# Two matmuls per weight tile, of 512 and 256 columns, in SwiGLU, output projection and gate of a hybrid trunk on one Trainium2 core

## The chip, the cores and the metric

The program runs on one NeuronCore of a Trainium2 chip. A core has five engines with queues of their own: TensorE (PE) multiplies matrices from SBUF into PSUM, VectorE (DVE) and ScalarE (ACT) read both memories, GpSimd (POOL) is used here on SBUF alone, and SyncE (SP) issues the DMAs. The metric is the device time of one execution in microseconds; lower is better.

## The reference

Two layers of a trunk over 256 tokens and 1024 features, all in float32. Each layer is

```
x += 1/2 SwiGLU_a(RMSNorm(x))              # 1024 -> 2 x 2816 -> 1024
u  = RMSNorm(x) @ W_in                     # 1024 -> 3072, the mixer: 8 heads of attention, Hyena convolution
x += W_out [RMSNorm(y_A) ; RMSNorm(y_B)] * g_out
x += 1/2 SwiGLU_b(RMSNorm(x))
x += sigmoid(RMSNorm(x) @ W_g) * (p[i] @ W_p)
```

and a last RMSNorm follows. `swiglu(h) = (silu(h @ w_gate) * (h @ w_up)) @ w_down`. Weights are read once: 192 MB in all.

## The kernel before

Activations lie transposed: features on the 128 partitions, the 256 tokens (T) in the free dimension, so x is eight tiles x[0..7] of 128x256. A weight matrix comes in tiles of 128x128, sixteen to a DMA of 1 MB (`raw`), in the order in which they are used.

float32 products are made from two rounded parts. Each operand is split into a high part and what remains, the low part: w = wh + wl, x = xh + xl. ACT casts eight weight tiles at a time to wh (L250), DVE subtracts to get wl (L253; in the mixer every third half goes to POOL), and six such halves of 8 tiles are in flight (`WBUFS`). The parts of an activation lie side by side in one tile of 128x512: `hl[:, :T]` high and `hl[:, T:]` low. `mm3` (L164) then issues three matmuls of 256 columns per weight tile, wh·xh, wh·xl and wl·xh (L165, L166, L167), which add up in 256 columns of a PSUM bank. Each matmul loads its weights anew.

PSUM is a pool `ps` of eight banks of 128x512. In SwiGLU a bank holds 256 columns of the gate and 256 of the up product of one block of 128 hidden features; the first two blocks (`heads`) are computed together, column by column of x, in four half-filled banks. 1/rms of the norm is known later than the products: it is spread over all partitions into `rb` and multiplied in on the way out of PSUM (L439 in DVE). Then follow silu on ACT (L442), gate times up on DVE (L445), the high part on ACT (L447) and the low part on DVE (L449). The down projection sums 22 tiles into one bank per column and DVE adds half of it to x (L480). The output projection is done in two parts of four tiles per column, for the attention and the Hyena half; each waits for its own 1/rms (`rna`, `rhy`), is multiplied by it (L886) and added to x (L887, on POOL for the first part, on DVE for the second). `prep` makes the parts xg of the next norm's input (ACT L329, DVE L331) and sums squares (ACT L314, POOL L317).

The order is set in the program: the products go to PE one weight tile after the other, and after every three weight tiles (`TICK`) each live `Fiber` is advanced by one step, so that the rest is recorded in small steps between the products. That order is kept as written on PE and ACT (`ORDERED`); DVE and POOL are ordered by the framework's scheduler. All engines run their queues in order.

Of the kernel before, what the change touches and what calls it, by code (L numbers as in the profile page):

```python
# [11 lines left out]
F32 = mybir.dt.float32  # L12
# [3 lines left out]
ALU = mybir.AluOpType  # L16
AX = mybir.AxisListType

P = 128
# [40 lines left out]
# columns of the packed per-partition parameters of one layer  # L60
# [15 lines left out]
def hybrid_trunk(ctx: ExitStack, tc: tile.TileContext, w, xT, pT, rpb, small, wf, zT, dft, idft, decay, out):  # L76
# [11 lines left out]
    psp = ctx.enter_context(tc.tile_pool(name="ps", bufs=8, space=bass.MemoryType.PSUM))  # L88
# [8 lines left out]

    def bank():
        return psp.tile([P, 512], F32, tag="ps", name=nm("ps"))
# [19 lines left out]
    class Fiber:  # L119
        """Work of several engines, emitted step by step between the products."""  # L120
# [43 lines left out]
    def mm3(o, lh, ll, rh, rl, start, stop):  # L164
        PE.matmul(o, lh, rh, start=start, stop=False)  # L165
        PE.matmul(o, lh, rl, start=False, stop=False)  # L166
        PE.matmul(o, ll, rh, start=False, stop=stop)  # L167
        if not Pace.inside:
            Pace.total += 1
            Pace.count += o.free_size() // T if hasattr(o, "free_size") else o.shape[-1] // T  # L170
            while Pace.count >= TICK:
                Pace.count -= TICK
                tick()

# [21 lines left out]
    # even times, odd times, and the latter's negative; real and imaginary parts  # L196
# [37 lines left out]
    def part(steps=1):  # L234
        """The next 8 weight tiles in their two 12-bit parts."""
        n = Stream.parted
        Stream.parted += 1
        while Stream.loaded < min(n // 2 + 2, DEPTH * PIECES):
            load()
        raw = Stream.raws[n // 2]  # L240
        h = whp.tile([P, HALF, P], F32R, tag="wh", name=nm("wh"))
        l = wlp.tile([P, HALF, P], F32R, tag="wl", name=nm("wl"))
        fb = Fiber(None)
        Stream.ready[n] = (h, l, fb)

        def go():
            k = HALF // steps
            for a in range(0, HALF, k):
                src = raw[:, n % 2 * HALF + a : n % 2 * HALF + a + k]
                S.copy(h[:, a : a + k], src)  # L250
                yield
                e = G if Stream.on_pool and n % Stream.on_pool == 0 else V
                e.tensor_sub(l[:, a : a + k], src, f(h[:, a : a + k]))  # L253
# [39 lines left out]
    class Inputs:  # L293
        """The two parts of g * x of the norm at hand."""
# [5 lines left out]
        def __getitem__(self, c):  # L300
            hl, fb = self.xs[c]
            fb.finish()
            return hl[:, :T], hl[:, T:]

    class Squares:
        """Sum of the squares of `n` blocks, in whatever order they come."""
# [27 lines left out]
    def onward(i, cg, c, before):  # L334
        """After `before`, which brings x[c] up to date, the next norm's input."""
        hl = t2(F32R, "xg")

        def go():
            yield from before
            yield  # L340
            yield from prep(i, cg, c, hl)

        scaled.append((hl, spawn(go())))

    def rsqrt(v):
        """v ** -0.5 of two columns by Newton's steps from the exponent's halving."""
# [18 lines left out]
    class Rstd:  # L365
        """1/rms of each token: `r`, tokens on partitions, and `dst`, on all partitions."""
# [58 lines left out]
    def ffn(i, cg_next, i_next):  # L425
# [5 lines left out]
        def gated(pg, pu, joint, hl):  # L431
            yield from rest(EV)
            yield from rs.wait()
            gu = t2(s="gu")
            if joint is None:
                V.tensor_mul(gu[:, :T], pg, rb)
                V.tensor_mul(gu[:, T:], pu, rb)
            else:
                V.tensor_tensor(v2(gu), v2(joint), rb2(), op=ALU.mult)  # L439
# [5 lines left out]
            V.tensor_mul(a, s, gu[:, T:])  # L445
            yield
            S.copy(hl[:, :T], a)  # L447
            yield
            V.tensor_sub(hl[:, T:], a, f(hl[:, :T]))  # L449
# [5 lines left out]
        heads = [bank()[:, :T] for _ in range(4)]  # L455
        for c in range(KD):
            xh, xl = xs[c]
            for o in heads:
                wh, wl = ws.next()
                mm3(o, wh, wl, xh, xl, c == 0, c == KD - 1)  # L460
        for j in (0, 2):
            start(heads[j], heads[j + 1], None)
        for ff in range(2, NF):
            b = bank()
            for o in (b[:, :T], b[:, T:]):
                product(o, ws, xs)
            start(None, None, b)
        ws = Tiles()
        new_norm()
        for c in range(KD):  # L470
            ps = bank()[:, :T]
            for k in range(NF):
                wh, wl = ws.next()
                hl, fb = act[k]
                fb.finish()
                mm3(ps, wh, wl, hl[:, :T], hl[:, T:], k == 0, k == NF - 1)
# [14 lines left out]
    def filter_steps(i):  # L491
# [96 lines left out]
        # sums and differences of the even and the odd times' spectra  # L588
# [22 lines left out]
    def mixer(i):  # L611
# [3 lines left out]
        def columns(between=None):  # L615
            """Two blocks of 128 columns of u from the next 16 weight tiles."""
# [7 lines left out]
        # values, tokens on partitions  # L624
# [36 lines left out]
        class QK:  # L661
            """Queries and keys of a pair of heads, the queries with zeros for the other head."""
# [25 lines left out]
        class Head:  # L688
            """One head's probabilities: the scores' softmax, then turned over."""
# [56 lines left out]
        def head_norm(src, sq, ch, hl):  # L746
            """The two parts of g * y, and its squares added up."""
# [21 lines left out]
        def conv(b, chans, res):  # L769
            """Short convolution of the two blocks of channels in a bank."""  # L770
# [66 lines left out]
        def spectral(a, ps):  # L837
            """The gated input's spectrum, frequencies on partitions, times the filter's."""
# [34 lines left out]
        def project(wo, c, parts):  # L873
            ps = bank()[:, :T]
            for k in range(4):
# [3 lines left out]
                mm3(ps, wh, wl, hl[:, :T], hl[:, T:], k == 0, k == 3)  # L879
            return ps  # L880

        def add(c, ps, st, e):
            yield from rest(EV)
            yield from st.wait()
            t = t1()
            V.tensor_mul(t, ps, st.dst)  # L886
# [71 lines left out]
    def ple(i, last, given):  # L958
# [22 lines left out]
        def update(c, ps):  # L981
            yield from rest(PLE_EV)
            yield from rs.wait()
            g = t1()
            V.tensor_mul(g, ps, rb)
# [27 lines left out]
        for c in range(KD):  # L1013
            ps = bank()[:, :T]
            product(ps, ws, xs)
# [80 lines left out]
def _rpb_index():  # L1096
    """Where the bias of (token of the query, token of the key) lies; the last place outside the window."""
# [7 lines left out]
def _tiles(wm):  # L1105
    """[K, M] -> [M tiles, K tiles, 128, 128]."""
# [97 lines left out]
```

## Time and profile before

| | us |
|---|---|
| runs | 1114.56, 1114.68, 1115.82 |
| median | 1114.68 |
| span of the profiled execution, first to last instruction | 1112.9 |
| PE busy | 1087.2 |
| DVE busy | 840.5 |
| ACT busy | 600.3 |
| POOL busy | 205.1 |
| mean granted TensorE clock | 0.996 of full |

The profile is one execution; its span leaves out what lies before the first and after the last instruction. In it the gate and up products of layer 0 run from 6 to 140 us, its down projection to 207, the mixer to 306, the output projection to 330, SwiGLU b to 525 and the gated input to 531; layer 1 follows with the same stages, and its last gate product ends at 1100.

In the profile's rows `L253 DVE ... wl<-raw,wh 128x1024` reads: line of the kernel, engine, operation, tile written and tiles read, shape. Timeline rows begin with the start and the duration in us; x2 and above are merged instructions. In the views by stretch each engine's busy time stands beside its number of instructions.

### The profile page before, as it was taken

Reading aid. Unit: us, or ns where it says so; the run is one execution under the profiler, and the core shown is the slowest. Engines: PE = TensorE matmul, PEld = TensorE weight load, DVE = VectorE, ACT = ScalarE, POOL = GpSimd, SP = SyncE. Lnnn points to the kernel's source line nnn. Section 1 sums busy time; section 2 is a strip of 40 time slices with the busy share of each in tenths; the row PEclk is TensorE's granted clock in tenths of the full one; section 3 lists DMA queues with packets and bytes.
Section 4 is the critical chain, followed back from the end, with each engine's and each line's share of the span. In section 5 each row is a group of like instructions: output and inputs, shape, how many; then the busy total and the mean of one; then the engine's idle time right before and its main releaser. Section 6 shows DMA issues by size and latency. Waiting matters only on the chain.

```text
span 1112.9 us, 21462 instructions
## 1 busy us (share of the span) xinstructions
PE 1087.2 (98%) x8828; PEld 1074.4 (97%) x8828; DVE 840.5 (76%) x1352; ACT 600.3 (54%) x1006; POOL 205.1 (18%) x182
## 2 busy tenths in 40 slices
PE   7999999999999999999999999999999999999996
PEld 7999999999999999999999999999989999999995
DVE  4988777798999766655878878677899986665554
ACT  6555455376746444444655455544855554444444
POOL 3000111544362000011100002125433700000111
PEclk9999999999999999999999999999999999999998
DMA  8565455454335555455455554454523464555421
GB/s 319 215 236 201 154 191 186 170 173 169 114 117 197 190 189 190 176 175 183 161 195 200 215 188 174 173 185 152 190 77 114 142 217 183 189 189 186 176 95 39
DMA packets 32994, 194.29 MB, mean 175 GB/s; under 512 B 3584, under 2 KB 6528, under 8 KB 10880
## 3 DMA queue, kind: packets, MB, share of 16 engines
q1 hardware_dynamic: 32896, 192.92, 48.4%
q8 instruction: 69, 1.13, 0.4%
q14 instruction: 29, 0.24, 0.1%
HBM read 191.86 MB, written 1.05 MB: 173 GB/s over the span
## 4 chain that ended last, share of the span: by engine, by line
PE 80%; DVE 11%; ACT 4%; issue 3%; DMA 1%; POOL 1%; SPq 0%; ACTq 0%; DVEq 0%; POOLq 0%
PE ps L166 26%; PE ps L167 26%; PE ps L165 26%; DVE wl L253 2%; ACT wh L250 2%; DMA raw<-in_w 1%; DVE rt L360 1%; DVE s L783 1%; DVE s L886 1%; DVE x L887 1%; ACT t L723 1%; DVE xg L331 0%; POOL acc L317 0%; ACT t L716 0%; DVE y L752 0%
## 5 line engine op out<-in xcount | busy, mean ns | idle before, releaser
L253 DVE TENSOR_TENSOR wl<-raw,wh 128x1024 fp32r<-128x1024 f32 (+1 forms) x328 | 410.9, 1257 | 193.7 <-ACT wh L250 191.7
L250 ACT CAST wh<-raw 128x1024 fp32r<-128x1024 f32 (+1 forms) x350 | 362.0, 1040 | 321.6 <-PE ps L166 226.8
L165 PE MATMUL ps<-xg,wh 128*128 128x256 f32 x1856 | 528.2, 285 | 5.9 <-ACT xg L1032 5.9
L166 PE MATMUL ps<-xg,wh 128*128 128x256 f32 x1856 | 527.5, 284 | 5.4 <-DVE xg L331 5.3
L167 PE MATMUL ps<-xg,wl 128*128 128x256 f32 x1856 | 526.9, 284 | 0.0
L166 PEld LDWEIGHTS ps<-xg,wh 128*128 128x128 f32 x1856 | 357.7, 193 | 7.2 <-DVE xg L331 6.3
L165 PEld LDWEIGHTS ps<-xg,wh 128*128 128x128 f32 x1856 | 357.8, 193 | 6.3 <-ACT xg L1032 5.9
L167 PEld LDWEIGHTS ps<-xg,wl 128*128 128x128 f32 x1856 | 357.7, 193 | 0.0
L167 PE MATMUL ps<-act,wl 128*128 128x256 f32 x704 | 199.4, 283 | 0.0
L165 PE MATMUL ps<-act,wh 128*128 128x256 f32 x704 | 199.4, 283 | 0.0
L166 PE MATMUL ps<-act,wh 128*128 128x256 f32 x704 | 199.4, 283 | 0.0
L317 POOL TENSOR_TENSOR acc<-acc,q 128x256 f32<-128x256 f32 x62 | 65.9, 1064 | 541.2 <-ACT q L314 524.8
L165 PEld LDWEIGHTS ps<-act,wh 128*128 128x128 f32 x704 | 135.2, 192 | 0.4
L166 PEld LDWEIGHTS ps<-act,wh 128*128 128x128 f32 x704 | 135.2, 192 | 0.4
L167 PEld LDWEIGHTS ps<-act,wl 128*128 128x128 f32 x704 | 135.2, 192 | 0.0
L439 DVE TENSOR_TENSOR gu<-ps,rb 128x512 f32<-128x512 f32 x80 | 55.0, 689 | 20.6 <-PE ps L167 19.0
L253 POOL TENSOR_TENSOR wl<-raw,wh 128x1024 fp32r<-128x1024 f32 x22 | 55.0, 2499 | 62.7 <-ACT wh L250 49.9
L566 POOL TENSOR_TENSOR t<-t,t 128x512 f32<-128x512 f32 x4 | 5.7, 1414 | 225.7 <-PE ps L167 121.0
L329 ACT ACTIVATE xg<-x,sm 128x256 fp32r<-128x256 f32 x56 | 28.1, 506 | 33.2 <-DVE x L480 14.0
L397 ACT ACTIVATE s<-ident,rl 128x128 fp32r<-128x128 f32 x24 | 8.3, 395 | 65.4 <-DVE rl L392 65.4
L442 ACT ACTIVATE s<-gu 128x256 f32<-128x256 f32 x88 | 35.9, 414 | 12.8 <-DVE gu L439 12.0
L449 DVE TENSOR_TENSOR act<-s,act 128x256 fp32r<-128x256 f32 x88 | 38.3, 444 | 0.0
(193 smaller groups left out, 1222.7 us busy)
## 6 DMA issues: line engine op xcount, KB each, us to landing
raw<-in_w SPq DMA_DIRECT2D x172, 1024.0 KB, 4.8
bias<-in_rpb SPq DMA_DIRECT2D x16, 256.0 KB, 2.8
raw<-in_w SPq DMA_DIRECT2D x4, 256.0 KB, 4.6
x<-in_xT SPq DMA_DIRECT2D x8, 128.0 KB, 4.8
raw<-in_w SPq DMA_DIRECT2D x2, 512.0 KB, 5.7
t<-in_wf SPq DMA_DIRECT2D x4, 256.0 KB, 5.4
dec<-in_decay SPq DMA_DIRECT2D x4, 256.0 KB, 5.4
out<-o SPq DMA_DIRECT2D x4, 256.0 KB, 2.4
```

The costliest lines, as they stand in the source:

```text
L165: PE.matmul(o, lh, rh, start=start, stop=False)
L166: PE.matmul(o, lh, rl, start=False, stop=False)
L167: PE.matmul(o, ll, rh, start=False, stop=stop)
L250: S.copy(h[:, a : a + k], src)
L253: e.tensor_sub(l[:, a : a + k], src, f(h[:, a : a + k]))
L317: G.tensor_add(self.ac, self.ac, q)
L329: S.activation(hl[:, :T], x[c], AF.Copy, scale=g)
L360: V.tensor_scalar(r[:, c], y[:, c], y[:, c], hv[:, c], op0=ALU.mult, op1=ALU.mult)
L439: V.tensor_tensor(v2(gu), v2(joint), rb2(), op=ALU.mult)
L442: S.activation(s, gu[:, :T], AF.Silu)
L449: V.tensor_sub(hl[:, T:], a, f(hl[:, :T]))
L723: S.activation(e[:, cs], e[:, cs], AF.Copy, scale=ri[:, tt : tt + 1])
```

## The change

A weight tile now takes two matmuls. `mm2` issues wh times the whole 128x512 tile [xh, xl], so that columns 0 to 255 of the bank hold wh·xh and columns 256 to 511 wh·xl, and then adds wl·xh, 256 columns wide, onto the second half. The two halves of the bank are summed on the way out. SwiGLU (gate, up, down), the output projection and the gate of the per-layer input use it; the mixer's columns, values, attention, transforms and the per-layer projection keep `mm3`. The low parts count for nothing less than before: the same three partial products are formed.

```diff
-    psp = ctx.enter_context(tc.tile_pool(name="ps", bufs=8, space=bass.MemoryType.PSUM))
+    psp = ctx.enter_context(tc.tile_pool(name="ps", bufs=4, space=bass.MemoryType.PSUM))
...
+    def pair():
+        return psp.tile([P, 2, 512], F32, tag="ps", name=nm("ps"))
     def bank():
-        return psp.tile([P, 512], F32, tag="ps", name=nm("ps"))
+        if not free:
+            b = pair()
+            free.extend((b[:, 1], b[:, 0]))
+        return free.pop()
...
+    def mm2(b, lh, ll, r, start, stop):
+        PE.matmul(b, lh, r, start=start, stop=False)
+        PE.matmul(b[:, T:], ll, r[:, :T], start=False, stop=stop)
+        paced()
+
+    def halves(dst, b):
+        if len(b.shape) == 3:
+            dst = v2(dst)
+        S.copy(dst, b[..., T:])
+        yield
+        V.tensor_add(dst, dst, b[..., :T])
...
-        def gated(pg, pu, joint, hl):
+        def gated(b, hl):
             yield from rest(EV)
+            gu = t2(s="gu")
+            yield from halves(gu, b)
             yield from rs.wait()
-            gu = t2(s="gu")
-            if joint is None:
-                V.tensor_mul(gu[:, :T], pg, rb)
-                V.tensor_mul(gu[:, T:], pu, rb)
-            else:
-                V.tensor_tensor(v2(gu), v2(joint), rb2(), op=ALU.mult)
+            G.tensor_tensor(v2(gu), v2(gu), rb2(), op=ALU.mult)
+            yield
             yield
             s = t1()
             S.activation(s, gu[:, :T], AF.Silu)
...
             def half_step(c=c, ps=ps):
                 yield from rest(EV)
-                V.scalar_tensor_tensor(x[c], ps, 0.5, x[c], op0=ALU.mult, op1=ALU.add)
+                for b in (ps[:, :T], ps[:, T:]):
+                    V.scalar_tensor_tensor(x[c], b, 0.5, x[c], op0=ALU.mult, op1=ALU.add)
...
         def add(c, ps, st, e):
             yield from rest(EV)
+            t = t1()
+            yield from halves(t, ps)
             yield from st.wait()
-            t = t1()
-            V.tensor_mul(t, ps, st.dst)
+            V.tensor_mul(t, t, st.dst)
             e.tensor_add(x[c], x[c], t)
...
         def update(c, ps):
             yield from rest(PLE_EV)
+            g = t1()
+            yield from halves(g, ps)
             yield from rs.wait()
-            g = t1()
-            V.tensor_mul(g, ps, rb)
+            V.tensor_mul(g, g, rb)
```

PSUM is handed out in four pairs of banks: a block of SwiGLU takes a pair (gate in one bank, up in the other), and `bank()` deals out the halves of a pair one after the other, so that a pair comes free when both halves have been read. The copy of the second half and its sum with the first don't wait for 1/rms; the multiplication by it does, and in SwiGLU it is POOL's.

On PE, in SwiGLU b of layer 0, two weight tiles of one block before the change (ps: PSUM, xg: the parts of g·x, wh and wl: the parts of the weights):

```order
L165 MATMUL ps_5053<-xg_4299,wh_4919 128x256
L166 MATMUL ps_5053<-xg_4299,wh_4919 128x256
L167 MATMUL ps_5053<-xg_4299,wl_4920 128x256
L165 MATMUL ps_5053<-xg_4334,wh_4919 128x256
L166 MATMUL ps_5053<-xg_4334,wh_4919 128x256
L167 MATMUL ps_5053<-xg_4334,wl_4920 128x256
```

and three weight tiles now:

```order
L191 MATMUL ps_4078<-xg_3674,wh_3915 128x512
L192 MATMUL ps_4078<-xg_3674,wl_3916 128x256
L191 MATMUL ps_4078<-xg_3689,wh_3915 128x512
L192 MATMUL ps_4078<-xg_3689,wl_3916 128x256
L191 MATMUL ps_4078<-xg_3714,wh_3915 128x512
L192 MATMUL ps_4078<-xg_3714,wl_3916 128x256
```

The 512 columns of xg pass wh in one matmul; 2368 of 8742 rows of PE are gone.

On DVE, at the same place, a block's work before:

```order
L439 TENSOR_TENSOR gu_5005<-ps_4918,rb 128x512
L253 TENSOR_TENSOR wl_4987<-raw_4804,wh_4986 128x1024
L445 TENSOR_TENSOR s_5032<-s_5019,gu_5005 128x256
L253 TENSOR_TENSOR wl_5022<-raw_4869,wh_5021 128x1024
L449 TENSOR_TENSOR act_4984<-s_5032,act_4984 128x256
```

and now, where gu_4214 goes to POOL (L473, times rb) and then to ACT between its first and its fourth row here:

```order
L201 TENSOR_TENSOR gu_4214<-gu_4214,ps_4146 128x512
L484 TENSOR_TENSOR act_4145<-s_4205,act_4145 128x256
L281 TENSOR_TENSOR wl_4232<-raw_4103,wh_4231 128x1024
L480 TENSOR_TENSOR s_4253<-s_4244,gu_4214 128x256
L484 TENSOR_TENSOR act_4199<-s_4253,act_4199 128x256
```

DVE's multiplication by rb has become the sum of the two halves.

On DVE in the output projection of layer 0, the steps from the first column of the Hyena part to the first xg before (s: the scaled column, rhy: its 1/rms):

```order
L886 TENSOR_TENSOR s_4268<-ps_4216,rhy_2757 128x256
L886 TENSOR_TENSOR s_4271<-ps_4199,rhy_2757 128x256
L887 TENSOR_TENSOR x_86<-x_86,s_4268 128x256
L887 TENSOR_TENSOR x_85<-x_85,s_4271 128x256
L886 TENSOR_TENSOR s_4287<-ps_4236,rhy_2757 128x256
L886 TENSOR_TENSOR s_4304<-ps_4258,rhy_2757 128x256
L887 TENSOR_TENSOR x_87<-x_87,s_4287 128x256
L887 TENSOR_TENSOR x_88<-x_88,s_4304 128x256
L331 SCALAR_TENSOR_TENSOR xg_4235<-x_86,sm,xg_4235 128x256
```

and now:

```order
L201 TENSOR_TENSOR s_3706<-s_3706,ps_3675 128x256
L923 TENSOR_TENSOR s_3694<-s_3694,rhy_2265 128x256
L923 TENSOR_TENSOR s_3706<-s_3706,rhy_2265 128x256
L924 TENSOR_TENSOR x_85<-x_85,s_3694 128x256
L924 TENSOR_TENSOR x_86<-x_86,s_3706 128x256
L201 TENSOR_TENSOR s_3736<-s_3736,ps_3675 128x256
L923 TENSOR_TENSOR s_3736<-s_3736,rhy_2265 128x256
L363 SCALAR_TENSOR_TENSOR xg_3689<-x_86,sm,xg_3689 128x256
```

Each column has one more row (L201), and the product with rhy now reads two tiles in SBUF.

More of the change, by code (lines that the diff above doesn't have):

```diff
@@ L96, in nm @@
         return f"{s}{uid[0]}"
+    free = []
+    def pair():
+        return psp.tile([P, 2, 512], F32, tag="ps", name=nm("ps"))
     def bank():
-        return psp.tile([P, 512], F32, tag="ps", name=nm("ps"))
+        if not free:
+            b = pair()
+            free.extend((b[:, 1], b[:, 0]))
+        return free.pop()
     def t2(dt=F32, s="t"):
@@ L167, in mm3, with paced @@
         PE.matmul(o, ll, rh, start=False, stop=stop)
+        paced(o.free_size() // T if hasattr(o, "free_size") else o.shape[-1] // T)
+    def paced(n=1):
         if not Pace.inside:
             Pace.total += 1
-            Pace.count += o.free_size() // T if hasattr(o, "free_size") else o.shape[-1] // T
+            Pace.count += n
             while Pace.count >= TICK:
@@ L300, in __getitem__, with both @@
         def __getitem__(self, c):
+            hl = self.both(c)
+            return hl[:, :T], hl[:, T:]
+        def both(self, c):
             hl, fb = self.xs[c]
             fb.finish()
-            return hl[:, :T], hl[:, T:]
+            return hl
     class Squares:
@@ L422, in product, with product2 @@
             mm3(o, wh, wl, xh, xl, c == 0, c == KD - 1)
+    def product2(b, ws, xs):
+        for c in range(KD):
+            wh, wl = ws.next()
+            mm2(b, wh, wl, xs.both(c), c == 0, c == KD - 1)
     def ffn(i, cg_next, i_next):
@@ L453, in start @@
             act.append((hl, spawn(gated(*a, hl))))
-        heads = [bank()[:, :T] for _ in range(4)]
+        heads = [pair() for _ in range(2)]
         for c in range(KD):
[L457 to L462, printed above, removed]
+            for b in heads:
+                for j in range(2):
+                    wh, wl = ws.next()
+                    mm2(b[:, j], wh, wl, xs.both(c), c == 0, c == KD - 1)
+        for b in heads:
+            start(b)
         for ff in range(2, NF):
[L464 to L467, printed above, removed]
+            b = pair()
+            for j in range(2):
+                product2(b[:, j], ws, xs)
+            start(b)
         ws = Tiles()
@@ L470, in ffn @@
         for c in range(KD):
-            ps = bank()[:, :T]
+            ps = bank()
             for k in range(NF):
@@ L873, in project @@
         def project(wo, c, parts):
-            ps = bank()[:, :T]
+            ps = bank()
             for k in range(4):
@@ L878, in project @@
                 fb.finish()
-                mm3(ps, wh, wl, hl[:, :T], hl[:, T:], k == 0, k == 3)
+                mm2(ps, wh, wl, hl, k == 0, k == 3)
             return ps
@@ L1013, in ple @@
         for c in range(KD):
-            ps = bank()[:, :T]
-            product(ps, ws, xs)
+            ps = bank()
+            product2(ps, ws, xs)
             if last:
```

2 lines of the change are left out of this document (1 added, 1 removed).

## The prediction

> **What bounds the kernel now.** I read the page first: busy time by engine and the slices, then the chain that ended last.
>
> ```profile
> PE 1087.2 (98%) x8828; PEld 1074.4 (97%) x8828; DVE 840.5 (76%) x1352; ACT 600.3 (54%) x1006; POOL 205.1 (18%) x182
> DVE  4988777798999766655878878677899986665554
> PEclk9999999999999999999999999999999999999998
> PE 80%; DVE 11%; ACT 4%; issue 3%; DMA 1%; POOL 1%; SPq 0%; ACTq 0%; DVEq 0%; POOLq 0%
> ```
>
> TensorE is busy in 98% of the span at nine tenths or more of its clock in every slice but the last; the chain is PE's for 80% and VectorE's for 11%. Busy time of pipelined matmuls says little about what one costs, so next comes the distance from start to start in the timeline of PE: first 256 columns (36 rows, first and last), then 512 columns (32 rows), then two 512s among 256s.
>
> ```profile
> 199.77 0.28 PE L166 MATMUL ps<-act,wh 128*128 128x256 f32 x1
> ...
> 203.97 0.28 PE L165 MATMUL ps<-act,wh 128*128 128x256 f32 x1
> 207.16 0.39 PE L165 MATMUL ps<-wh,xg 128*128 128x512 f32 x1
> ...
> 214.19 0.39 PE L166 MATMUL ps<-wl,xg 128*128 128x512 f32 x1
> 120.72 0.40 PE L551 MATMUL ps<-t,s 128*128 128x512 f32 x1
> 120.95 0.40 PE L552 MATMUL ps<-t,s 128*128 128x512 f32 x1
> 121.19 0.28 PE L165 MATMUL ps<-xg,wh 128*128 128x256 f32 x1
> ...
> 121.89 0.28 PE L165 MATMUL ps<-xg,wh 128*128 128x256 f32 x1
> ```
>
> 35 steps in 4.20 us are 120.0 ns each; 31 steps in 7.03 us are 226.8 ns. The extra 256 columns cost 106.8 ns, so of each matmul 13.2 ns is independent of its columns. That is what this change can remove. In the mixed stretch two 512s and six 256s take 1.17 us, as 2 x 226.8 + 6 x 120.0 = 1174 ns has it.
>
> Tiles that go from three matmuls to two: gate/up 1408 (of the 1856 on xg; 320 belong to the mixer's columns and stay, 128 are the gate), down 704, output projection 128, gate 128; together 2368.
>
> ```profile
> L165 PE MATMUL ps<-xg,wh 128*128 128x256 f32 x1856 | 528.2, 285 | 5.9 <-ACT xg L1032 5.9
> L165 PE MATMUL ps<-act,wh 128*128 128x256 f32 x704 | 199.4, 283 | 0.0
> L165 PE MATMUL ps<-y,wh 128*128 128x256 f32 x128 | 36.4, 285 | 0.0
> ```
>
> Where PE is not alone in setting the pace is read by stage: three gate/up stretches (SwiGLU a of layer 0, SwiGLU a of layer 1, SwiGLU b of layer 0), then the two stretches from the output projection to the heads of SwiGLU b.
>
> ```profile
> 43.00:140.00 97.00, 97.00 (x804) 96.65 (x803) 82.06 (x129) 52.48 (x83) 3.79 (x3) 1.00 0.54 195
> 545.00:684.00 139.00, 139.00 (x1154) 138.64 (x1154) 114.33 (x189) 75.16 (x124) 10.49 (x10) 1.00 0.53 188
> 346.00:462.00 116.00, 116.00 (x969) 116.00 (x969) 81.78 (x125) 57.17 (x87) 0.00 (x0) 1.00 0.53 190
> 310.00:345.00 35.00, 32.08 (x264) 31.47 (x263) 33.97 (x64) 21.06 (x39) 24.55 (x20) 1.00 0.42 146
> 860.00:890.00 30.00, 27.65 (x229) 27.24 (x228) 29.31 (x56) 15.65 (x29) 22.74 (x18) 1.00 0.43 155
> ```
>
> The columns are PE, PEld, DVE, ACT, POOL busy. In gate/up DVE idles 15 us of 97 in layer 0 (the Hyena filter runs there), 25 of 139 in layer 1, 34 of 116 in SwiGLU b. Around 310 to 345 DVE is busy 33.97 of 35.00 and PE has holes: there VectorE is the bound.
>
> **The change part by part.**
>
> *Matmuls.* A tile costs 226.8 + 120.0 = 346.8 ns instead of 360.0: 2368 x 13.2 ns = 31.3 us if PE sets the pace everywhere. No row shows 512 and 256 strictly in turn. Bounds from the mixed rows: after the 512s three 256s take 0.34 us, 113 ns each, so a pair could cost 340 (47 us saved); the dearest step there, 240 ns, plus 120 is 360 (nothing saved). The sum over the whole mixed stretch decides for 13.2. A page's rule is weaker here: the Trainium skill, "TensorE: Matmul & The Clock Gate", Back-to-back issue gap, gives columns / 2.4 plus 2.5 ns. By it the sum of this term would be 5.9 us; the rows above, 13.2 ns, disagree and decide.
>
> *The new way out of PSUM in SwiGLU.* For each of 88 blocks of hidden columns, one DVE multiply from PSUM becomes an ACT copy of one half, a DVE add of the other, and the multiply moves to POOL.
>
> ```profile
> L976 ACT COPY t<-ps 128x512 f32<-128x512 f32 x8 | 4.6, 582 | 0.5 <-PE ps L167 0.5
> L850 POOL TENSOR_TENSOR t<-t,t 128x512 f32<-128x512 f32 x8 | 10.3, 1295 | 11.3 <-DVE t L845 6.8 <-DVE ri L719 4.6
> 404.18 0.69 DVE L439 TENSOR_TENSOR gu<-ps,rb 128x512 f32<-128x512 f32 x1 [0.32 <-PE ps L167]
> 405.19 1.22 DVE L253 TENSOR_TENSOR wl<-raw,wh 128x1024 fp32r<-128x1024 f32 x1 [0.32 <-ACT wh L250]
> 406.34 0.42 DVE L445 TENSOR_TENSOR s<-s,gu 128x256 f32<-128x256 f32 x1
> 408.06 1.23 DVE L253 TENSOR_TENSOR wl<-raw,wh 128x1024 fp32r<-128x1024 f32 x1 [1.31 <-ACT wh L250]
> 409.20 0.42 DVE L449 TENSOR_TENSOR act<-s,act 128x256 fp32r<-128x256 f32 x1
> 409.94 0.69 DVE L439 TENSOR_TENSOR gu<-ps,rb 128x512 f32<-128x512 f32 x1 [0.32 <-PE ps L167]
> ```
>
> DVE's own work per block stays (an add of 0.69 for a multiply of 0.69). ACT gains 0.58 us per block of 5.55 (16 x 346.8 ns), which its idle time hides (it is busy in 54% or less of the gate/up rows). The add waits for that copy, and DVE's next split of weights stands behind the add. POOL gains 1.30 us per block, 88 x 1.30 = 114 us, and idles there; the price is what POOL's work does to DVE:
>
> ```profile
> 314.05 2.59 POOL L253 TENSOR_TENSOR wl<-raw,wh 128x1024 fp32r<-128x1024 f32 x1
> 314.30 1.41 DVE L886 TENSOR_TENSOR s<-ps,rna 128x256 f32<-128x256 f32 x4
> 315.63 2.09 DVE L253 TENSOR_TENSOR wl<-raw,wh 128x1024 fp32r<-128x1024 f32 x1
> 337.02 2.83 DVE L887 TENSOR_TENSOR x<-x,s 128x256 f32<-128x256 f32 x2
> ```
>
> While POOL ran its 2.59 us, DVE ran four multiplies with an input in PSUM at 0.35 us each, undisturbed; the split of weights that followed, with both inputs in SBUF, took 2.09 instead of 1.22 and ended 1.1 us after POOL did. So a DVE instruction with two SBUF inputs and a POOL instruction exclude each other. The Trainium skill, "SBUF — State Buffer", Who interferes with whom, says the same and that the later one blocks fully; the trace agrees.
>
> So each multiply on POOL takes up to 1.30 us from DVE. From the period above (5.76 us) DVE is busy 1.23 + 1.22 + 0.69 + 0.42 + 0.42 = 3.98; with POOL 5.28 of 5.55. In SwiGLU b it fits. In layer 0's SwiGLU a 17 blocks bring 22 us and PE leaves 3.6 us less, against 15 us of idle: 10.6 us short. In layer 1, 22 blocks bring 28.6 + 5.1 against 24.7: 9 short. Cover is the lead of split weights, a ring of six halves (2.77 us each); most of the time it is full, since ACT's casts wait for PE to free a buffer:
>
> ```profile
> ACT wh L250 <- PE ps L166: 226.8, 155, 3.0
> ```
>
> Five halves ahead are 13.9 us, but layer 0 starts with less, since in the second slice of the page (28 to 56 us) DVE is busy nine tenths or more. Ends: 0 and 20 us of new PE stalls. I take 4 for layer 0 and 1.5 for layer 1, nearer the covered end, since the lead is worth more than the shortfall once it has built up.
>
> *Output projection.* Two projections of 8 columns of tiles per layer: each gains an ACT copy and a DVE add, and the multiply by 1/rms now reads SBUF twice. The stretch 309.9 to 343.7 us in groups:
>
> ```profile
> L886 DVE TENSOR_TENSOR s<-ps,rhy 128x256 f32<-128x256 f32 x8 | 3.1, 411 | 0.0
> L253 POOL TENSOR_TENSOR wl<-raw,wh 128x1024 fp32r<-128x1024 f32 x3 | 8.4, 2797 | 0.1
> L887 POOL TENSOR_TENSOR x<-x,s 128x256 f32<-128x256 f32 x8 | 7.6, 980 | 1.2 <-DVE s L886 1.2
> L317 POOL TENSOR_TENSOR acc<-acc,q 128x256 f32<-128x256 f32 x7 | 6.9, 986 | 5.2 <-ACT q L314 5.0
> DVE wl L253 <- ACT wh L250: 0.7, 2, 0.4
> PE ps L166 <- DVE xg L331: 2.9, 3, 1.3
> ```
>
> DVE waits for others only 0.7 us there and PE already waits 2.9 us for DVE's xg: what is added to DVE comes out at PE. 16 adds back to back (four in 1.41) are 5.6 us. The 16 multiplies, until now free to run beside POOL, must find the port free, with POOL busy some 23 us of 34. Ends per layer: 5.6 - 0.7 = 4.9, and 5.6 + 5.6 = 11.2. I take 6.2, near the low end, since the adds may now run where the multiplies did: 12.4 us for two layers. The casts of xg on ACT queue behind the new copies (16 x 0.4 us), but ACT waits for DVE there, so they are late only with it. And 128 + 56 tiles of this stretch (projections and most of the heads) don't see their 13.2 ns: 2.4 us of the 31.3 lost.
>
> *PSUM in four pairs of banks instead of eight banks.* In SwiGLU a bank pair is emptied without waiting for 1/rms, which frees it earlier: nothing lost. In the mixer a pair is free when both its halves are, about one bank later than before; PE waits nowhere on a bank in the trace of before. Ends 0 and 6 us, by DVE's density there; I take 1.5.
>
> *Down projection and gate.* Down adds one DVE step of 0.42 per column, 8 per SwiGLU, where DVE idles half the time: hidden by that. Gate: copy and add per column; 0.5 us where the next heads wait. At the end of the program the last gate column has no cover:
>
> ```profile
> 1099.95 0.42 DVE L985 TENSOR_TENSOR s<-ps,rb 128x256 f32<-128x256 f32 x1 [0.96 <-PE ps L167]
> ```
>
> After it the chain is serial to the end; before it now stand a copy and an add: 1.0 us.
>
> *Sum.* 31.3 - 2.4 - 12.4 - 5.5 - 1.5 - 0.5 - 1.0 = 8.0 us. The profiled span is 1112.9; 1.8 us lie around it to the median of 1114.68. Span 1104.9, time 1106.7; I say 1106.
>
> **The rivals.**
>
> *A cleaner gain, 1094.* The adds slip beside POOL's instructions as the multiplies did, the output stretch costs 2 us a layer, the lead covers gate/up: 31.3 - 2.4 - 4 - 1 - 3 = 21 us. For it: DVE instructions with a PSUM input ran undisturbed beside POOL. Against: DVE's density from 310 to 345.
>
> *The port becomes the bound, slower, 1124.* Each block's silu on ACT waits for POOL, POOL for a pause of DVE, DVE's next product for the silu; the weight casts stand behind that silu in ACT's queue. It decides from 0.27 us of lost time per block (5.55 less 5.28); at 0.5 us the period is 5.78, 80 x 0.23 = 18 us more than forecast: 1106 + 18 = 1124. For it: the layer 0 budget. Against: lead and 34 us of idle DVE in SwiGLU b.
>
> *A pair costs what three cost, 1130.* If each step from 512 to 256 columns costs the dear 240 ns and the next 120, PE saves nothing, the stalls in gate/up fade with the spare time DVE keeps, and the output stretch, tail and pairs remain: 1114.7 + 12.4 + 1.0 + 1.5 = 1130. Against: the mixed rows add up. By the Trainium skill's gap rule, named above, nearly nothing hangs on a single matmul either, and 5.9 us would come off these 1130; that case shares the chance of this rival.
>
> *The costs eat the gain exactly, 1112.5 to 1117.* Stalls of 14 us instead of 5.5.
>
> **How the numbers follow.** Forecast (1099 to 1112.4) 0.50; cleaner gain (1087 to 1099) 0.18; even 0.13; port bound 0.13; pair not cheaper 0.06. A measurement here tells 0.2% (2.2 us) from nothing, so faster 0.68, same 0.13, slower 0.19. The range 1089 to 1122 leaves out the last of both ends; the likeliest case's own is 1099 to 1112.
>
> **What would show it.** Right: pairs of matmuls at about 347 ns in down and SwiGLU b, no PE wait from 380 to 460 us; PE waits on xg around the output projections up from 3 to about 9 us a layer; DVE splits of weights beside POOL's gu above 2 us. Wrong: pairs at 360 ns, or ACT's silu waiting for POOL with PE waiting for wl in gate/up in both layers, or the output stretch no longer than now.

## The result, and the profile after

The changed kernel takes 1218.68 us (median; 1215.49 to 1221.44) against 1114.62: 1.0929 times as long, interval 1.0910 to 1.0949. That is 104 us slower, far outside the range of 1089 to 1122. Two executions of the kernel with the changed output projection alone (below) were disturbed, 1312.51 and 3719.36 us; its times leave them out.

The page of the changed kernel: busy time, the clock by slices, and the chain that ended last.

```profile
PE 1104.8 (91%) x6460; PEld 963.8 (79%) x6460; DVE 929.1 (76%) x1424; ACT 655.7 (54%) x1142; POOL 347.5 (29%) x270
PEclk9999889999999999999999999999999999999997
PE 40%; DVE 12%; ACT 3%; issue 2%; POOL 0%; ACTq 0%; DVEq 0%
```

PE has 6460 instructions instead of 8828, 2368 fewer. But it is busy 91% of a longer span instead of 98%, and its clock falls to eight tenths in two early slices; the mean granted clock is 0.974 instead of 0.996. The chain was followed back only to 513 us, so its shares add up to 57%; of what was followed PE has 40 in 57, or 70%, instead of 80%. So look at what PE waits for: before the change, then after it (us in total, times, longest).

```profile
PE ps L165 <- ACT xg L1032: 5.9, 1, 5.9
PE ps L166 <- DVE xg L331: 5.3, 5, 1.3
```

```profile
PE ps L191 <- DVE x L516: 20.9, 14, 2.1
PE ps L191 <- DVE xg L363: 10.7, 6, 3.6
PE ps L191 <- DVE gu L201: 8.7, 4, 3.5
PE ps L191 <- DVE act L484: 7.3, 4, 2.4
PE ps L175 <- DVE t L745: 6.0, 4, 2.6
PE ps L191 <- ACT rna L437: 5.5, 2, 3.1
```

The first row is the news. `x L516` is the half step after a column of the down projection. PE waits 14 times for it, three or four times in each of four down projections, where it waited for nothing before. One such place in the timeline (last SwiGLU, columns 2 and 3):

```profile
1123.57 0.40 PE L191 MATMUL ps<-act,wh 128*128 128x512 f32 x1
1123.80 0.28 PE L192 MATMUL ps<-act,wl 128*128 128x256 f32 x1
1124.12 0.88 DVE L516 SCALAR_TENSOR_TENSOR x<-ps,x 128x256 f32<-128x256 f32 x2 [0.23 <-PE ps L192]
1125.05 0.50 PE L191 MATMUL ps<-act,wh 128*128 128x512 f32 x1 [0.97 <-DVE x L516]
```

The two half steps read column 2's bank and end at 1125.00; PE goes on at 1125.05. Yet PE had been in column 3, in another bank, for five weight tiles. And the half steps themselves had waited for PE until its last matmul into that other bank was done (1123.80 + 0.28). So neither hides the other: PE stops, DVE reads, PE goes on. The program says why. On PE, the first SwiGLU's down projection, three weight tiles of column 1, and on DVE the half steps of column 0 (in brackets the engine for whose signal an instruction waits):

```
L191 MATMUL ps296_1523<-act78_431,wh285_1463 128x512
L192 MATMUL ps296_1523<-act78_431,wl286_1464 128x256
L191 MATMUL ps296_1523<-act91_495,wh285_1463 128x512 [waits DVE_49]
L192 MATMUL ps296_1523<-act91_495,wl286_1464 128x256
L191 MATMUL ps296_1523<-act107_568,wh285_1463 128x512

L516 SCALAR_TENSOR_TENSOR x0_85<-ps296_1523,x0_85 128x256 [waits PE_49]
L516 SCALAR_TENSOR_TENSOR x0_85<-ps296_1523,x0_85 128x256 [waits DVE_49]
```

`ps296` is the pair, one tile of two banks. The framework orders work by tile, so a matmul that is written down after the half steps waits for them, though they read the other bank. The half steps are written down a tick or two after their column (a tick is three weight tiles), inside the next column's products, so PE stops inside column 1. Every place where `bank()` deals out halves can have this: down, mixer (`t L745`), projections (`rna L437`, where ACT reads the spread 1/rms out of a neighbouring bank).

Start-to-start times over all matmuls, with the waits that the program carries laid beside them, give PE's lost time: 150 us after, 28 before. 65 us in 52 places end with a reading of a pair's other bank; 15 us wait for a pair to come free; 32 us are other data (17 before); 34 us are steps without any wait (8 before), mostly at a lower clock; some 4 us belong to none of these. The 122 us of new lost time less the 20 that fewer matmuls save (see below) make 102 of the 104.

Such steps at the lower clock look like this:

```profile
139.12 0.63 PE L191 MATMUL ps<-xg,wh 128*128 128x512 f32 x1
139.55 0.42 PE L192 MATMUL ps<-xg,wl 128*128 128x256 f32 x1
139.76 0.63 PE L191 MATMUL ps<-xg,wh 128*128 128x512 f32 x1
```

Here a pair of matmuls takes 640 ns instead of 350. The granted clock is 0.50 from 138.55 to 148.79 us; there are eleven such stretches in the middle of the program, of 3.4 to 10.2 us, 51 us in all. One lies in or right behind 13 of the 18 waits of 2.0 us or more there, and behind none of the shorter ones. By the Trainium skill, "TensorE: Matmul & The Clock Gate", Wait — 56ns, not 53.3ns?, a cold matmul starts every N / 1.2 ns, 427 + 213 for a pair; the rows agree.

The third thing is ACT's wait for POOL, with the groups of POOL's multiply and DVE's splits:

```profile
ACT s L477 <- POOL gu L473: 146.5, 77, 3.7
```

```profile
L473 POOL TENSOR_TENSOR gu<-gu,rb 128x512 f32<-128x512 f32 x88 | 144.8, 1651 | 352.3 <-DVE gu L201 305.0
L281 DVE TENSOR_TENSOR wl<-raw,wh 128x1024 fp32r<-128x1024 f32 (+1 forms) x328 | 452.8, 1382 | 148.0 <-ACT wh L278 144.9
```

POOL's multiply takes 1651 ns, not 1295; the splits 1382 on average, 1257 before. In the trace 71 splits overlap one of these multiplies and take 1818 ns on average; the other 257 take 1261. ACT's silu waits 77 times, 1.9 us each, with the rest of ACT's queue behind it.

### The profile page after: what moved, and what is told of

It reads as the page before. It is cut to its first block, busy times and chain, and to the rows that moved or that the text cites. A ratio compares the mean times of both kernels' runs of the same rounds, so it can differ in the third digit from the quotient of the medians.

```text
span 1216.1 us, 17140 instructions
## 1 busy us (share of the span) xinstructions
PE 1104.8 (91%) x6460; PEld 963.8 (79%) x6460; DVE 929.1 (76%) x1424; ACT 655.7 (54%) x1142; POOL 347.5 (29%) x270
## 4 chain that ended last, share of the span: by engine, by line
PE 40%; DVE 12%; ACT 3%; issue 2%; POOL 0%; ACTq 0%; DVEq 0%
PE ps L191 23%; PE ps L192 11%; DVE wl L281 4%; PE ps L175 2%; PE ps L177 2%; PE ps L176 2%; ACT wh L278 2%; DVE x L516 1%; DVE s L201 1%; DVE s L923 1%; DVE rt L392 1%; DVE s L819 0%; DVE gu L201 0%; DVE t L745 0%; DVE xg L363 0%
## 5 line engine op out<-in xcount | busy, mean ns | idle before, releaser
L191 PE MATMUL ps<-xg,wh 128*128 128x512 f32 x1536 | 557.6, 406 | 34.6 <-DVE xg L363 10.7
L281 DVE TENSOR_TENSOR wl<-raw,wh 128x1024 fp32r<-128x1024 f32 (+1 forms) x328 | 452.8, 1382 | 148.0 <-ACT wh L278 144.9
L191 PEld LDWEIGHTS ps<-xg,wh 128*128 128x128 f32 x1536 | 294.9, 192 | 112.0 <-DVE xg L363 10.1
L191 PE MATMUL ps<-act,wh 128*128 128x512 f32 x704 | 255.1, 405 | 29.4 <-DVE x L516 20.9
L473 POOL TENSOR_TENSOR gu<-gu,rb 128x512 f32<-128x512 f32 x88 | 144.8, 1651 | 352.3 <-DVE gu L201 305.0
L191 PEld LDWEIGHTS ps<-act,wh 128*128 128x128 f32 x704 | 134.7, 191 | 67.9 <-DVE x L516 24.2
L349 POOL TENSOR_TENSOR acc<-acc,q 128x256 f32<-128x256 f32 x62 | 61.0, 984 | 339.9 <-ACT q L346 337.1
L175 PE MATMUL ps<-xg,wh 128*128 128x256 f32 x320 | 92.3, 288 | 9.2 <-DVE t L745 6.0
L176 PE MATMUL ps<-xg,wh 128*128 128x256 f32 x320 | 91.4, 286 | 0.0
L480 DVE TENSOR_TENSOR s<-s,gu 128x256 f32<-128x256 f32 x88 | 43.2, 500 | 39.2 <-ACT s L477 39.2
L175 PEld LDWEIGHTS ps<-xg,wh 128*128 128x128 f32 x320 | 62.1, 194 | 10.5 <-DVE t L745 6.8
L176 PEld LDWEIGHTS ps<-xg,wh 128*128 128x128 f32 x320 | 62.1, 194 | 0.1
L361 ACT ACTIVATE xg<-x,sm 128x256 fp32r<-128x256 f32 x56 | 28.1, 508 | 63.1 <-DVE x L516 43.1
## 6 DMA issues: line engine op xcount, KB each, us to landing
x<-in_xT SPq DMA_DIRECT2D x8, 128.0 KB, 5.0
```

The lines of the kernel that those rows point to most:

```text
L191: PE.matmul(b, lh, r, start=start, stop=False)
L349: G.tensor_add(self.ac, self.ac, q)
L361: S.activation(hl[:, :T], x[c], AF.Copy, scale=g)
L473: G.tensor_tensor(v2(gu), v2(gu), rb2(), op=ALU.mult)
```

## The experiments

"Own banks" means that each bank is a tile of its own again, eight of them; a SwiGLU block then takes two and is emptied in two copies and two adds of 256 columns. The ratios are taken against runs of the kernel before in the same sitting, with medians of 1114.6 to 1115.1 us.

| kernel | us | against before |
|---|---|---|
| changed | 1218.7 | 1.0929 |
| e5: a pair for each down column | 1192.5 | 1.0689 |
| e2: multiply on DVE | 1199.5 | 1.0755 |
| e1: own banks | 1169.0 | 1.0484 |
| e4: own banks, three matmuls | 1172.0 | 1.0511 |
| e12: own banks, silu two ticks later | 1146.7 | 1.0294 |
| e3: own banks, multiply on DVE | 1137.9 | 1.0206 |
| e6: e3, projection and gate as before | 1116.6 | 1.0007 |
| e10: e6, three matmuls | 1126.1 | 1.0096 |
| e9: e6, first gate/up as before | 1107.6 | 0.9923 |
| e7: before, two matmuls in down alone | 1112.3 | 0.9971 |
| e8: before, two matmuls in the output projection alone | 1134.1 | 1.0167 |

The stretches, each from its first product to the next one's, in us (the gate of layer 0 counts with gate/up a of layer 1; the rest of layer 1 is not listed):

| | before | changed | e1 | e3 | e6 | e9 |
|---|---|---|---|---|---|---|
| gate/up a, 0 | 134.2 | 148.6 | 141.8 | 133.4 | 134.0 | 133.9 |
| down a, 0 | 67.1 | 78.2 | 77.1 | 72.7 | 73.2 | 65.8 |
| mixer, 0 | 99.3 | 108.9 | 100.1 | 100.2 | 100.4 | 99.3 |
| output projection, 0 | 24.0 | 31.3 | 31.0 | 31.0 | 25.1 | 25.0 |
| gate/up b, 0 | 131.1 | 132.2 | 131.1 | 131.0 | 127.7 | 128.0 |
| down b, 0 | 63.3 | 70.2 | 67.3 | 62.3 | 63.4 | 63.3 |
| gate/up a, 1 | 153.6 | 163.1 | 156.1 | 155.9 | 151.3 | 151.3 |
| down a, 1 | 67.0 | 76.3 | 75.4 | 67.1 | 66.6 | 66.4 |

**Own banks (e1).**

```diff
     def pair():
-        return psp.tile([P, 2, 512], F32, tag="ps", name=nm("ps"))
+        return [bank(), bank()]
     def bank():
-        if not free:
-            b = pair()
-            free.extend((b[:, 1], b[:, 0]))
-        return free.pop()
+        return psp.tile([P, 512], F32, tag="ps", name=nm("ps"))
```

> Every PSUM bank is a tile of its own again (eight of them; a SwiGLU block takes two, so it is emptied by two copies and two adds of 256 columns); two matmuls per weight tile and the multiply on POOL stay. Theory 'shared tile' (a matmul into one bank of a pair waits until the reads of the other bank are done): the 52 waits of PE on readers of the neighbouring bank, 65 us, go, and with them some 25 of the 34 us of steps at the low clock behind them: 1218.7 - 90 = 1129, range 1115 to 1145. Rival 'POOL in the chain' (silu on ACT waits 146 us for POOL's product and holds up copies and casts): PE's waits only change their names, 1195 or more.

1169.0, 49.7 us less, between the two expected ranges: the shared tile is real, and it is not the whole. No wait on a neighbouring bank is left and the mixer is back at 100.1 us. It is not 90 less: other waits took the place, above all one for the last parts of act at the start of the down projections (the last row; ACT's wait above it). Of PE's lost time, reckoned as above, 101 us are left. The 65 us on neighbouring banks are gone, and waits for a free bank fell from 15 to 4; but waits for data rose from 32 to 65 (8 to 22 of them for act). The steps without a wait fell only from 34 to 27, where 25 had been expected to go: PE still stops long enough, and the clock still stands at half for 55 us in the middle of the program.

```profile
ACT s L475 <- POOL gu L471: 163.6, 75, 5.8
```

```profile
PE ps L188 <- DVE act L482: 21.0, 6, 5.5
```

**A pair for each column of down (e5).** The cleanest of the tests, since not one instruction more or less is computed.

```diff
         for c in range(KD):
-            ps = bank()
+            ps = pair()[:, 0]
```

> The changed kernel with one line different: each column of the down projection takes a pair of banks for itself and uses one bank of it, so that the neighbour is never written while it is read; the instructions are the same. 'Shared tile': the 13 waits of the down projections on half_step's readings (22 us) and the slow-clock steps after them (some 7 us) go: 1218.7 - 29 = 1190, range 1183 to 1197. If only the number of banks counted, wasting four of eight would help nothing or harm: 1215 or more.

1192.5, 26 us less and inside the range expected of the shared tile: half of the pairs' storage is wasted and the kernel is faster. The row of 20.9 us is gone from PE's waits; the next ones stay as they were:

```profile
PE ps L191 <- DVE xg L363: 10.7, 6, 3.6
PE ps L191 <- DVE gu L201: 8.5, 4, 3.5
```

**The multiply on DVE (e2, and with own banks e3).**

```diff
-            G.tensor_tensor(v2(gu), v2(gu), rb2(), op=ALU.mult)
+            V.tensor_tensor(v2(gu), v2(gu), rb2(), op=ALU.mult)
```

> The multiply of gu by 1/rms goes from POOL to DVE, all else as in the changed kernel, pairs of banks included. 'Shared tile': only the 15 us in which a block waits for a pair whose emptying stood behind a silu go, and a few us of slow clock: 1195 to 1208. 'POOL in the chain': the larger part of the 104 us goes, 1150 or less.

> Both of the former: banks of their own and the multiply on DVE. 'Shared tile': 90 us from the banks and up to 15 from the multiply, 1105 to 1130, and at most 15 us under the kernel with banks alone. 'POOL in the chain': much the same as with the multiply on DVE alone.

With pairs 1199.5, 19.2 us less, which is what the shared tile leaves to it. With own banks 1137.9, 31.1 less: more than the 15 expected, and outside the 1105 to 1130. What the pairs cost had hidden part of what POOL costs; turned round, own banks gain 49.7 us with the multiply on POOL and 61.6 with it on DVE. The rows with own banks and DVE's multiply:

```profile
ACT s L475 <- DVE gu L471: 69.4, 47, 3.7
```

```profile
PE ps L188 <- DVE act L482: 8.7, 4, 5.1
```

ACT waits 69 us instead of 164, PE for act 8.7 instead of 21.0.

**Silu later (e12).** Is it POOL's claim on DVE, or the place of silu in ACT's order?

```diff
             G.tensor_tensor(v2(gu), v2(gu), rb2(), op=ALU.mult)
-            yield
-            yield
+            yield from rest(4)
```

> Banks of their own with the multiply on POOL (1169.0), but silu stands two steps (six weight tiles, 2.1 us of PE) later in ACT's order. There ACT waits 164 us for POOL's products, 75 times 2.2 us, and the casts of weights stand behind. 'ACT's order': most of that wait goes, casts come earlier, and much of the 31 us that the multiply on DVE gained comes back: 1140 to 1155. 'Length of the chain': PE pays at the start of the down projections, where it waits 22 us for the last act parts, and a later silu only lengthens that: 1169 to 1180.

1146.7: 22 of the 31 us come back with the multiply still on POOL. ACT's wait at silu falls from 164 to 21 us, and although silu stands later, the last act parts come earlier. Part of the wait has moved on to ACT's next step, the high part of act, which waits for DVE's product (31 us in e1, the first row):

```profile
ACT act L480 <- DVE s L478: 30.9, 29, 2.2
```

```profile
ACT s L474 <- POOL gu L471: 20.9, 13, 4.2
ACT act L479 <- DVE s L477: 106.4, 60, 4.3
```

```profile
PE ps L188 <- DVE act L481: 14.0, 4, 6.1
```

Both waits together fall from 194 to 127 us (107 in e3). So most of POOL's price hangs on where silu stands in ACT's order, and is ACT's queue standing still behind a step whose input is late; the 9 us left to e3 are the longer chain and the port together, not told apart.

**Output projection and gate as before (e6), the output projection alone (e8, e11).**

```diff
-                mm2(ps, wh, wl, hl, k == 0, k == 3)
+                mm3(ps, wh, wl, hl[:, :T], hl[:, T:], k == 0, k == 3)
...
-            t = t1()
-            yield from halves(t, ps)
             yield from st.wait()
-            V.tensor_mul(t, t, st.dst)
+            t = t1()
+            V.tensor_mul(t, ps, st.dst)
```

> Banks of their own and the multiply on DVE, but output projection and gate back with three matmuls and the evacuation of before. The output projection takes 31.0 us a layer with two matmuls and took 24.0 with three: 14 us come back, and 2 to 4 at the gate: 1137.9 - 17 = 1121, range 1116 to 1125. If the stretch were slow for another reason (DVE's load from SwiGLU's adds), less than 5 us come back.

The gate's lines change in the same way. 1116.6, 21.3 us less; the stretch falls from 31.0 to 25.1 us, and gate/up b after it from 131.0 to 127.7, which had not been expected.

> The kernel before with two matmuls in the output projection alone, own banks: by the prediction's term the adds and the port cost 6.2 us a layer and 128 tiles save nothing: 1114.7 + 12.4 = 1127; by the stretches of the kernels run so far (31.0 against 24.0 us) 14 us: 1128.5. Range 1124 to 1132. If the stretch is only slow together with SwiGLU's change, 1113 to 1118.

1134.1, 19.1 us more than before, also past the expected range.

> The kernel before with two matmuls in the output projection alone once more, for its profile: 1133 to 1135, PE in the stretch of the projections and of the next heads waits some 19 us more than before. 'Port': DVE is busy for all of the stretch, and the multiplies by 1/rms beside POOL take up to 1 us. 'Order': DVE stands idle while ACT's copies or casts of xg are late.

1134.5. The stretches now last 30.0 and 29.4 us, 5.4 to 6.0 more than before, and gate/up b behind them 1.8 and 4.9 more (132.9 and 135.1 us). Another 1.8 us lie in the very first gate/up products, which nothing of the change touches, beside a half-clock stretch at 29 us; the reason is open. DVE by groups, from 306 to 331 us before the change and from 308 to 338 us here:

```profile
L886 DVE TENSOR_TENSOR s<-ps,rna 128x256 f32<-128x256 f32 x8 | 2.9, 413 | 0.0
```

```profile
L899 DVE TENSOR_TENSOR s<-s,rna 128x256 f32<-128x256 f32 x8 | 8.4, 1074 | 0.0
L897 DVE TENSOR_TENSOR s<-s,ps 128x256 f32<-128x256 f32 x11 | 4.3, 409 | 0.0
L263 DVE TENSOR_TENSOR wl<-raw,wh 128x1024 fp32r<-128x1024 f32 x4 | 5.1, 1272 | 1.4 <-ACT wh L260 1.4
323.39 0.41 DVE L899 TENSOR_TENSOR s<-s,rna 128x256 f32<-128x256 f32 x1
329.69 2.40 POOL L263 TENSOR_TENSOR wl<-raw,wh 128x1024 fp32r<-128x1024 f32 x1 [5.07 <-ACT wh L260]
329.96 2.75 DVE L899 TENSOR_TENSOR s<-s,rna 128x256 f32<-128x256 f32 x2
```

The eight multiplies of the attention's part, each followed by POOL's addition to x, take 1074 ns on average with both inputs in SBUF and took 413 from PSUM; beside them stand eleven adds of 409. The one that ran between two instructions of POOL took 0.41 us, two beside POOL's split 2.75. DVE is busy for 28.1 of the 30 us and its longest idle time is 1.4 us, so it is not the 'order' that was expected as the other case. By these rows the port put 8 x 0.66 = 5.3 us a layer on DVE and the sixteen adds 6.5 (an estimate): the port is half of it, the adds themselves the other half. The Trainium skill, "SBUF — State Buffer", Who interferes with whom, says that DVE's second SBUF input shares a port with POOL; the rows agree, and the PSUM adds beside them at 409 ns are not touched.

**Three matmuls again (e4 with own banks, e10 on e6).**

```diff
-        PE.matmul(b, lh, r, start=start, stop=False)
+        if start:
+            PE.matmul(b, lh, r, start=True, stop=False)
+        else:
+            PE.matmul(b[:, :T], lh, r[:, :T], start=False, stop=False)
+            PE.matmul(b[:, T:], lh, r[:, T:], start=False, stop=False)
```

> As with banks of their own, but the 512 columns of xg go through in two matmuls of 256 except at the start of a sum: 2112 weight tiles take three matmuls again, into the same halves of a bank, and all evacuation stays. In the changed kernel a pair of matmuls took 352 ns from start to start against 360 for three of 256, so 2112 x 8 ns = 17 us slower than banks of their own with two matmuls if PE sets the pace there; 28 us by the 13.2 ns of the prediction; 0 to 5 us if waits for ACT and DVE set the pace.

> As the kernel with two matmuls in SwiGLU alone (1116.6), but the 512 columns go through as twice 256 except at the start of a sum: 1904 weight tiles with three matmuls again. At 352 against 360 ns, 1904 x 8 = 15 us slower, 1131, if PE sets the pace; with banks of their own and POOL's multiply only 3 of 17 us showed, since PE waited anyway, so the least is 1118.

3.0 us (little more than the spread of the runs) and 9.5 us slower, of 17 and 15 that the matmuls take longer. In e4 PE's lost time falls from 101 to 84 us, in e10 from 46 to 40: a slower PE waits less. Where others set the pace, a matmul saved is a wait gained.

**Down alone (e7).**

```diff
-                mm3(ps, wh, wl, hl[:, :T], hl[:, T:], k == 0, k == NF - 1)
+                mm2(ps, wh, wl, hl, k == 0, k == NF - 1)
...
-                V.scalar_tensor_tensor(x[c], ps, 0.5, x[c], op0=ALU.mult, op1=ALU.add)
+                for b in (ps[:, :T], ps[:, T:]):
+                    V.scalar_tensor_tensor(x[c], b, 0.5, x[c], op0=ALU.mult, op1=ALU.add)
```

> The kernel before with two matmuls in the down projection alone: 704 weight tiles, no copy on ACT, one more half step on DVE per column. At the 8.6 ns per tile that the pairs gave in the changed kernel 704 x 8.6 = 6.1 us less: 1108.6; at the predicted 13.2 ns 9.3 us less: 1105.4. If waits take it back, 1114 to 1116.

1112.3, a ratio of 0.9971 (0.9959 to 0.9982): 2.7 us less. The pairs take 352.6 ns there, 7.4 x 704 = 5.2 us less on PE; about half came off. In one profile each, 2.5 us of new lost time are spread over the program; they have no one place.

**All of SwiGLU but the first gate/up (e9).** The kernel e6 with

```diff
-            b = pair()
+            b = bank() if first else pair()
             for j in range(2):
-                product2(b[j], ws, xs)
+                if first:
+                    product(b[:, j * T : (j + 1) * T], ws, xs)
+                else:
+                    product2(b[j], ws, xs)
```

and the evacuation of before in that first SwiGLU.

> Two matmuls in SwiGLU alone, with banks of their own and the multiply on DVE, but gate and up of the very first SwiGLU as before (there DVE also runs the Hyena filter, and with two matmuls the down projection behind it waited 5.2 us for the last act parts). Against the kernel that has two matmuls there too (1116.6): 6 us of that down projection come back, gate and up there lose nothing (134.0 with, 134.2 without): 1110.6, range 1107 to 1113. If the late act parts have another cause than that stretch, 1115 to 1118.

1107.6 us, a ratio of 0.9923 (0.9911 to 0.9936). It beats both kernels: 7 us under before, 111 under the change. Its page has PE at 97% and no slice but the last has a lower clock:

```profile
PE 1076.2 (97%) x7068; PEld 979.8 (89%) x7068; DVE 893.8 (81%) x1510; ACT 638.2 (58%) x1138; POOL 206.8 (19%) x182
PEclk9999999999999999999999999999999999999998
```

The first down projection falls from 73.2 us in e6 to 65.8, so its act parts had been late because of that stretch. That they were late because DVE also runs the Hyena filter there is likely, but not shown.

## Why the prediction was wrong

In the terms of its sum:

| term | predicted, us | measured, us | from |
|---|---|---|---|
| matmuls (31.3 less the 2.4 not seen at the projections) | -28.9 | -20.4 (2368 x 8.6 ns; pairs of 351.4 ns) | trace of the change |
| PSUM pairs | +1.5 (0 to 6) | +49.7 (with DVE's multiply 61.6) | change less e1 |
| gate/up stalls, POOL | +5.5 (0 to 20) | +31.1 (with pairs 19.2) | e1 less e3 |
| output projection, gate and tail | +13.9 | +21.3 | e3 less e6 |
| of these the output projection | +12.4 (9.8 to 22.4) | +19.1 | e8 less before |

From before to e6 stand 1.9 us, and 1.9 + 21.3 + 31.1 + 49.7 = 104.0. These are differences along one way from before to the change, so they add up to the result by construction; another order shares out pairs and POOL otherwise, as the brackets show. The 1.9 us hold what is left of the matmuls' saving in SwiGLU: 2112 pairs of 352.1 ns save 17 us, and PE's lost time, 46 us instead of 28, takes 18 back.

*The step that failed is "PSUM in four pairs of banks".* It asked when a pair comes free for its next owner, and took "PE waits nowhere on a bank in the trace of before" as evidence. But the change made a dependency that the old program doesn't have, so no trace of before could show it. The half steps were "hidden" by DVE's idle time; that DVE was idle was right (busy 40.47 of 72.00 us in the last down projection), and beside the point, since PE waited for their end, not for DVE's capacity. The prediction asked who waits behind an added instruction in DVE's queue, and not who waits for the tile that it reads. The waits stood in the built program (the row with the bracket above).

*Gate/up stalls: right mechanism, wrong size and wrong victim.* The rival "the port becomes the bound" had silu on ACT wait for POOL and gave it 18 us on top of the 5.5, 23.5 in all; it is 31. It expected late casts and PE waiting for wl. That did not happen: a half of wl was ready at least 3.4 us before its first matmul from 31 us on. What came late was what else stands in ACT's queue: the copies that empty PSUM (PE waits 8.7 us for the adds behind them, `gu L201`) and the last act parts before each down projection. "ACT gains 0.58 us per block, which its idle time hides" counted ACT's time and not its order. The sign "splits beside POOL's gu above 2 us" came true for 36 of the 71 splits that overlap one.

*Output projection: the stretch was right, the neighbourhood missed.* The adds and the port were to cost 6.2 us a layer; the stretches are 5.4 and 6.0 us longer. Of the remaining 8 us 6.7 lie behind them, in the next gate and up products, whose xg come late. PE's waits for xg came to 10.7 us in all, not 9 a layer.

*Matmuls: between the two bounds.* No row showed 512 and 256 in strict turn, and the value taken was too good. The timeline of the changed kernel has two rhythms: 30 weight tiles in 10.60 us (353.3 ns) and 35 in 12.14 us (346.9 ns; the predicted 346.8).

```profile
44.32 0.40 PE L191 MATMUL ps<-xg,wh 128*128 128x512 f32 x1
...
54.92 0.40 PE L191 MATMUL ps<-xg,wh 128*128 128x512 f32 x1
...
1144.16 0.39 PE L191 MATMUL ps<-act,wh 128*128 128x512 f32 x1
...
1156.30 0.39 PE L191 MATMUL ps<-act,wh 128*128 128x512 f32 x1
```

A rhythm holds until the next stop of PE; what chooses it stays open. The mean of undisturbed pairs, 351.4 ns, makes 8.6 ns of each matmul saved: more than the 2.5 of the Trainium skill's rule weighed in the prediction ("TensorE: Matmul & The Clock Gate", Back-to-back issue gap), less than the 13.2 of the rows. That two replace three is worth it where PE sets the pace: e9 kept 7.4 us of 1760 x 7 = 12.3 (its pairs take 353 ns).

*The range* was built from one surprise at a time, and it ended at 1122, below the 1124 and 1130 of two of its own rivals. Three terms failed together and on the same side, since a stopped PE also loses its clock (some 25 us of the 150) and each was bounded by rows of a program that does not have the new waits.

## What to carry to other kernels

Before changing how a buffer is cut into tiles, list the instructions that read one part while another part is written: if the framework orders by tile, each is a new wait, and the old trace cannot show it, while the built program's waits can. An engine with idle time is not free if it runs its queue in order: price an added operation by what stands behind it while its input is late, and place it late enough in the queue. Take a saving stage by stage: here it paid where the evacuation had room (SwiGLU b, down) and cost 19 us where VectorE was full.

## What the runs showed of the hardware

Alternating 512 and 256 columns have two stable rhythms, 353.3 and 346.7 ns a pair, that change only at stops; why is open.

In the trace of the changed kernel the granted clock has only the values 1.00 and 0.50, and its half-clock stretches in the middle of the program last 3.4, 6.8 or 10.2 us. There 13 of 18 waits from 2.0 to 3.8 us had one, all five above 3.0 us among them, and no shorter wait. That is no threshold: in e7 a wait of 1.2 us at 825 us has one behind it (0.50 from 826.88 to 830.29).

POOL's multiply of 128x512 with a broadcast input takes 1651 ns on average in the changed kernel, against 1295 for its plain one before (least, median and greatest):

```profile
L850 POOL TENSOR_TENSOR t<-t,t x8: 1275/1300/1309, 277.6 to 829.9; 128x512 f32<-128x512 f32 x8
L473 POOL TENSOR_TENSOR gu<-gu,rb x88: 1281/1408/2535, 41.8 to 1098.0; 128x512 f32<-128x512 f32 x88
```

Its shortest is as short as the plain one, so the broadcast alone costs nothing that shows.
